# The seven merged products of a four-block scheme, laid between the plain row tiles of the group before them, with bank sums started from copies instead of added at the eviction

## The chip, the cores and the metric

The kernel runs on one core of a Trainium2 chip. The metric is the device time of one execution in microseconds (us), median over runs. The engines are named as in the profile: PE (TensorE matmul) and PEld (its weight load), DVE (VectorE), ACT (ScalarE), POOL (GpSimd) and SP (SyncE, which here only issues transfers). Banks are PSUM banks of 128 x 512 fp32.

## The reference

One layer of a hybrid decoder on 256 tokens (and 16 meta tokens in front of them) with model width 2048 and hidden width 8192, all in fp32:

```
proj  = rmsnorm(x) @ w_in                      # q, k, v, gates of two branches
y     = sigmoid(gate_fox) * (fox(proj) @ w_o_fox) + sigmoid(gate_gla) * (gla(proj) @ w_o_gla)
h     = x + y @ w_out                          # "gemm of y" below
x2    = rmsnorm(h)
out   = h + square(relu(x2 @ w1)) @ w2         # the MLP: ff1 makes a, ff2 gathers into h
```

## The kernel before

**Arithmetic.** An fp32 product is made of three matmuls in fp32r. A tile of weights comes by DMA from SP's queue as `raw` (512 KB, 128 x 1024, a ring of five buffers). ACT casts it into the upper half of a `w` tile (the hi part), DVE subtracts to make the lower half (the lo part), and PE multiplies hi by the token tile's hi and lo parts, then lo by its hi part. `cut` is this pair of ACT and DVE instructions; `w` is a ring of five tiles for the whole kernel, so a cast waits until PE has done with the tile that lies five cuts back in its slot. Token tiles (`x2`, `a`) are kept already split.

**Stages.** The part that the change touches starts at 752 us: the out-projection of `y` in 16 columns j (`gemm2`), each with `add_residual` and the making of `x2`. Then the MLP in four groups of 2048 hidden columns. A group has two ff1 pairs (`x2` to hidden columns of `a`) and two ff2 pairs (`a` gathered into `h`). The last group has one ff1 pair, followed by `token_rows`, a last `hidden` and ordinary column products. That makes 13 pairs, counted here as index 0 to 12: index % 4 is 0 or 1 for ff1, 2 or 3 for ff2.

**A pair** (`two_wide`) makes two row tiles f = 0, 1 of 512 output columns for the two token tiles t = 0, 1 in four banks: `by`, `bx` for f = 0, `bz`, `bv` for f = 1. For the first four of the 16 k blocks it uses a scheme of seven products instead of eight: their weights are differences of weight tiles (made on DVE by `merge` into `ha` and `hb`) and their token operands are sums of token tiles (`s_x2`, `s_a`, made by `token_sums`). The other twelve k blocks are twelve `plain` tiles, two products of six matmuls each. One pair is 186 matmuls of 128 x 512. Three intermediate sums (`m1`, `m5`, `u3`) are copied out of banks by `snap` and added on DVE when the row tile is evicted. In the program's text the seven products and the plain tiles `plain(1,4)`, `plain(1,6)`, `plain(0,4)`, `plain(0,6)` of the same pair alternate, then eight plain tiles follow.

**Evictions.** `hidden` (ff1) adds the kept sum (`added`, DVE), applies relu and square (ACT), transposes 32 x 32 blocks on DVE and sends the result through memory: four DMAs `there<-turn`, one DMA `turn<-there`, then a split into `a` (`turned_parts`, one ACT cast and one DVE subtract per token half). For the first row tile of a group it also makes `s_a`. These steps are put behind numbers of later weight cuts: `behind.append([slot, ...])` counts them down at each cut (`made`). The `turn` tiles are a pool of two buffers, here called A and B; the temporary of `token_sums` is one of them too. `gathered` (ff2) adds into `ht`, and in the last groups turns as well.

**Order.** A scheduler works from the program's text, the waits and its own table of costs, and writes a fixed order for each engine; the DMA issues of a queue go out in order, and a waiting instruction holds whatever is behind it on its engine.

Of the kernel before, what the change touches and what calls it, by code (L numbers as in the profile page):

```python
# [16 lines left out]
P = 128  # L17
# [55 lines left out]
def trunk(ctx: ExitStack, tc: tile.TileContext, hT, w_small, w_all, consts, w_alpha2, out):  # L73
# [162 lines left out]
    def turn(rows, then, both, into=None, slot=10, reload=None):  # L236
# [13 lines left out]
        behind.append([slot, away])  # L250
        if reload:
            behind.append([slot, reload])
        behind.append([slot + 2, lambda: nc.scalar.dma_start(back, there)])
        behind.append([slot + 4, lambda: then(back.rearrange("p (c t j r) -> p j t c r", c=4, t=2, r=32))])
# [770 lines left out]

    acc2 = gat.tile([P, NT], F32, tag="acc", name="acc2", bufs=1)
    for j in range(KT):
# [7 lines left out]
        if j == 4:  # L1035
            g4 = gained[:, 0 : 4 * NT].rearrange("p (j t c r) -> p j t c r", j=4, t=2, r=32)
            token_sums(s_x2, lambda i, t: g4[:, 2 * i : 2 * i + 2, t], gained[:, 4 * NT :])
        if j % 4 == 3:
            nc.scalar.dma_start(kept[:, NT * (j - 3) : NT * (j + 1)].rearrange("p (j t) -> p j t", t=NT),
                                ht[:, j - 3 : j + 1, :])  # L1040
    r2 = gat.tile([P, 2], F32, name="r2", bufs=1)
# [30 lines left out]
    def added(dst, ps, more):  # L1072
        if more is None:
            return ps
        nc.vector.tensor_tensor(dst, ps, more, op=ALU.add)
        return dst

    def hidden(a, b, pt, more=(None, None), slot=10):
# [4 lines left out]
        def part(t):  # L1083
            nc.scalar.activation(u[:, t, :], added(u[:, t, :], pt[t], more[t]), AF.Relu, scale=r2[:, t : t + 1])
# [9 lines left out]
        turn([lambda t=t: part(t) for t in range(2)], ready, both, slot=slot)  # L1094

    def gathered(g, b, pt, more):
# [3 lines left out]
        for r, ps, m in zip(rs, pt, more):  # L1100
            if g == 0:
                if m is None:
                    nc.scalar.copy(r, cells(ps))
                else:
                    nc.vector.tensor_tensor(r, cells(ps), cells(m), op=ALU.add)
            else:
                nc.vector.tensor_tensor(r, cells(ps), r, op=ALU.add)
                if m is not None:
                    nc.vector.tensor_tensor(r, cells(m), r, op=ALU.add)
# [11 lines left out]
        turn([lambda r=r: r for r in rs], add, turn_tile(), reload=reload)  # L1121

    def fetch(dst, c0, k0):
        nc.sync.dma_start(dst.rearrange("p (c k m) -> p c k m", k=2, m=P),
                          w_all[c0 : c0 + 4, :, k0 * P : (k0 + 2) * P].rearrange("c p (k m) -> p c k m", m=P))

    def fetched(c0, k0):
        raw = wp.tile([P, HK * P], F32, tag="raw", name=nm("raw"), bufs=RAW)
        fetch(raw, c0, k0)
        return raw  # L1130

    def cut(raw):
        hi, lo = (t.rearrange("p k m -> p (k m)").rearrange("p (k c m) -> p k c m", k=2, m=P) for t in pair())
        r = raw.rearrange("p (c k m) -> p k c m", k=2, m=P)
        copied = nc.scalar.copy(hi, r).ins  # L1135
        nc.vector.tensor_tensor(lo, r, hi.bitcast(F32), op=ALU.subtract)  # L1136
        made(copied, 1)
        return [t.rearrange("p k c m -> p k (c m)") for t in (hi, lo)]

    def two_wide(x, sums, evict, between=None, split_order=False):  # L1140

        f1 = chunk[0]
        f2 = f1 + 4
        chunk[0] += 8
        begun = set()
        even = len(pairs_done) % 2 == 0
        pairs_done.append(f1)
        pools = (px, px, px, px) if even else (pg, pg, pg, px)
# [44 lines left out]
        if between:  # L1193
            between()
# [219 lines left out]
```

## Time and profile before

| what | value |
|---|---|
| median of three runs (1529.9, 1529.77, 1533.42) | 1529.9 us |
| time of the profiled execution | 1535.58 us |
| its span, from the first to the last instruction | 1533.9 us |
| mean granted clock of TensorE | 0.995 |
| gemm of `y`, by the starts of matmuls | 752.10 to 837.44 us |
| the 13 pairs (2422 matmuls of 128 x 512) | 837.44 to 1388.61 us |
| `token_rows` and the columns of the last group from `x2` | 1388.61 to 1431.4 us |
| the columns of the last group from `a`, and the end | 1431.4 to 1533.9 us |

In a row of groups of instructions the columns are: line, engine, operation, out<-in, shapes, how often; then busy us in total, mean ns of one; then the idle time of the engine just before them and what ended it. A timeline row gives start, length, engine, line, operation, and in brackets an idle time before it with the instruction whose end released it. A matmul of 128 x 512 has a record of 0.38 us, though the next one starts 0.22 us after it: PE overlaps them, so the pace is read from starts.

### The profile page before, as it was taken

How to read it: one execution, taken by the hardware profiler on the slowest of the kernel's cores; microseconds unless marked ns; L12 is line 12 of the kernel's file. 1: busy time of each engine (PE TensorE's matmuls, PEld its weight loads, DVE VectorE, ACT ScalarE, POOL GpSimd, SP SyncE). 2: the span in 40 equal slices, each digit the busy share in tenths (PEclk: the TensorE clock that was granted, in tenths of full speed). 3: DMA queues.
4: the chain of work that ended last, by engine and by line, in shares of the span. 5: the costliest groups of instructions: out<-in, count | busy, mean ns of one | idle time of the engine just before them, and what ended most of it. 6: DMA issues, size and time to landing. Idle time of an engine off the chain costs nothing.

```text
span 1533.9 us, 22711 instructions
## 1 busy us (share of the span) xinstructions
PE 1513.7 (99%) x8536; PEld 1340.6 (87%) x8536; DVE 1110.9 (72%) x1515; ACT 837.0 (55%) x1213; POOL 126.1 (8%) x198
## 2 busy tenths in 40 slices
PE   9999999999999999999999999999999999999997
PEld 8999999999998888888998878888788888888897
DVE  7898858586665454546788788777887788786765
ACT  7766444555555434444666466556654665455563
POOL 5012010021101000000011000000000000110022
PEclk9999999999999999999999999999999999999999
DMA  9545545465455566666664788667766678888562
GB/s 320 173 151 177 181 163 190 156 216 170 165 169 189 198 209 219 219 206 218 219 236 157 223 274 260 207 199 224 232 216 200 214 243 261 289 259 268 187 201 95
DMA packets 222898, 320.32 MB, mean 209 GB/s; under 512 B 11786, under 2 KB 188564, under 8 KB 222660
## 3 DMA queue, kind: packets, MB, share of 16 engines
q1 hardware_dynamic: 202116, 289.75, 58.0%
q10 hardware_dynamic: 20496, 27.99, 5.7%
q8 instruction: 67, 1.10, 0.3%
q0 software_dynamic: 176, 1.12, 0.2%
q14 instruction: 43, 0.35, 0.1%
HBM read 303.09 MB, written 15.74 MB: 208 GB/s over the span
## 4 chain that ended last, share of the span: by engine, by line
PE 79%; DMA 8%; DVE 6%; ACT 3%; issue 2%; ACTq 0%; POOL 0%; SPq 0%; POOLq 0%; DVEq 0%
PE ps L191 15%; PE ps L192 8%; PE bx L1156 7%; PE pt L226 5%; PE pt L225 5%; PE pt L224 5%; PE bz L1156 5%; PE by L1156 5%; PE bv L1156 5%; PE psa L196 4%; PE psa L200 4%; PE psa L198 4%; DMA raw<-w_all_dram 3%; DMA turn<-there 2%; DVE w L1136 2%
## 5 line engine op out<-in xcount | busy, mean ns | idle before, releaser
L134 DVE TENSOR_TENSOR w<-raw,w 128x1024 fp32r<-128x1024 f32 x222 | 273.1, 1231 | 103.1 <-ACT w L133 97.6
L133 ACT CAST w<-raw 128x1024 fp32r<-128x1024 f32 x222 | 232.6, 1049 | 98.2 <-PE psa L200 31.0
L1136 DVE TENSOR_TENSOR w<-raw,w 128x1024 fp32r<-128x1024 f32 x182 | 222.4, 1241 | 81.7 <-ACT w L1135 79.9
L1135 ACT CAST w<-raw 128x1024 fp32r<-128x1024 f32 x182 | 187.6, 1047 | 114.5 <-PE bx L1156 45.6
L191 PE MATMUL ps<-x,w 128*128 128x512 f32 x607 | 206.0, 383 | 0.0
L178 DVE TENSOR_TENSOR w<-raw,w 128x1024 fp32r<-128x1024 f32 x92 | 113.1, 1230 | 110.7 <-ACT w L177 108.8
L196 PE MATMUL psa<-x,w 128*128 128x272 f32 x640 | 181.7, 285 | 0.0
L200 PE MATMUL psa<-x,w 128*128 128x272 f32 x640 | 179.7, 282 | 0.0
L198 PE MATMUL psa<-x,w 128*128 128x272 f32 x624 | 175.9, 282 | 0.0
L192 PE MATMUL ps<-x,w 128*128 128x256 f32 x607 | 166.6, 274 | 0.0
L177 ACT CAST w<-raw 128x1024 fp32r<-128x1024 f32 x92 | 96.3, 1046 | 119.6 <-PE pt L226 113.2
L191 PEld LDWEIGHTS ps<-x,w 128*128 128x128 f32 x607 | 114.0, 188 | 19.3
L196 PEld LDWEIGHTS psa<-x,w 128*128 128x128 f32 x640 | 120.2, 188 | 0.2
L200 PEld LDWEIGHTS psa<-x,w 128*128 128x128 f32 x640 | 120.2, 188 | 0.1
L198 PEld LDWEIGHTS psa<-x,w 128*128 128x128 f32 x624 | 117.4, 188 | 0.0
L192 PEld LDWEIGHTS ps<-x,w 128*128 128x128 f32 x607 | 114.0, 188 | 0.0
L1135 ACT CAST w<-ha 128x1024 fp32r<-128x1024 f32 x52 | 54.4, 1047 | 78.4 <-DVE ha L1179 63.2
L191 PE MATMUL ps<-y,w 128*128 128x512 f32 x256 | 85.4, 380 | 0.0
L224 PE MATMUL pt<-w,x 128*128 128x512 f32 x224 | 85.2, 381 | 0.0
L225 PE MATMUL pt<-w,x 128*128 128x512 f32 x224 | 85.2, 380 | 0.0
L226 PE MATMUL pt<-w,x 128*128 128x512 f32 x224 | 85.2, 380 | 0.0
L1156 PE MATMUL bx<-w,x 128*128 128x512 f32 x336 | 82.8, 383 | 0.0
(402 smaller groups left out, 3095.6 us busy)
## 6 DMA issues: line engine op xcount, KB each, us to landing
raw<-w_all_dram SPq DMA_DIRECT2D x499, 512.0 KB, 4.4
there<-turn ACTq DMA_DIRECT2D x76, 128.0 KB, 3.5
turn<-there ACTq DMA_DIRECT2D x19, 512.0 KB, 6.3
raw<-w_all_dram SPq DMA_DIRECT2D x26, 256.0 KB, 3.5
ha<-w_all_dram SPq DMA_DIRECT2D x13, 512.0 KB, 6.7
hb<-w_all_dram SPq DMA_DIRECT2D x13, 512.0 KB, 4.3
raw<-w_all_dram SPq DMA_DIRECT2D x8, 384.0 KB, 6.5
h<-hT_dram SPq DMA_DIRECT2D x8, 275.0 KB, 6.5
```

Of the source, the lines that this page charges most:

```text
L133: copied = nc.scalar.copy(hi[:, k, :], r).ins
L134: nc.vector.tensor_tensor(lo[:, k, :], r, hi[:, k, :].bitcast(F32), op=ALU.subtract)
L191: nc.tensor.matmul(steps(ps), hi, steps(row(x)), start=first, stop=False)
L192: nc.tensor.matmul(steps(ps[:, 0:NT]), lo, steps(x[:, 0, :]), start=False, stop=last)
L196: nc.tensor.matmul(steps(ps[:, X_LO]), hi, steps(x_lo[:, k]), start=first, stop=False, skip_group_check=True)
L198: nc.tensor.matmul(steps(ps[:, 0:NA]), lo, steps(x_hi[:, k]), start=False, stop=last and hi is None, skip_group_check=True)
L200: nc.tensor.matmul(steps(ps[:, 0:NA]), hi, steps(x_hi[:, k]), start=False, stop=last, skip_group_check=True)
L224: nc.tensor.matmul(steps(ps), xh, steps(hi), start=(k == 0), stop=False)
L225: nc.tensor.matmul(steps(ps), xh, steps(lo), start=False, stop=False)
L1135: copied = nc.scalar.copy(hi, r).ins
L1136: nc.vector.tensor_tensor(lo, r, hi.bitcast(F32), op=ALU.subtract)
L1156: nc.tensor.matmul(steps(ps), l, steps(r), start=ps.tensor.name not in begun, stop=last and k == 1 and n == 2, skip_group_check=True)
```

## The change

`two_wide` becomes `pair_of`, which returns two lists: the seven steps of the scheme and the twelve plain tiles. A loop runs the plain tiles of one pair, and behind those numbered (2, 3, 4, 6, 8, 9, 10), or (1, 2, 3, 5, 7, 8, 9) where index % 4 is 2, it runs one step of the *next* pair. The first pair's seven steps go behind columns j = 8 to 14 of the gemm of `y`. Bank `y` starts as an ACT copy of bank `x` after the first product; `z` and `v` start as DVE sums of bank `x` and the copy `m5`. The kept sums `m1` and `u3` and the additions at the eviction go. All fetched tiles come from the ring `raw`; merged weights go to a ring `hold` of three. The numbers of cuts behind which an evicted tile is sent, fetched back and split change from 10, 12, 14 to 8, 11, 14 (8, 10, 12 for the last group's f = 1; 5, 7, 9 for 6, 8, 10 at the last `hidden`).

The core of the diff:

```diff
+        def step1():
+            r11, got["12"] = fetched(f1, 0), fetched(f2, 0)
+            w = cut(r11)
+            got["t1"] = merged(got["12"], r11)
+            product("x", own(0, 0), w, True)
+            nc.scalar.copy(bk("y"), bk("x"))
+        def step2():
+            got["22"] = fetched(f2, 2)
+            w = cut(got["t1"])
+            got["t2"] = merged(got["22"], got["t1"])
+            product("v", summed(0), w, True)
+            got["t3"] = merged(got["22"], got["12"])
+            got["m5"] = fp.tile([P, 512], F32, tag="m5", name=nm("m5"))
+            nc.scalar.copy(got["m5"], bk("v"))
+        def step3():
+            product("x", summed(1), cut(got["t2"]))
+            nc.vector.tensor_tensor(bk("z"), bk("x"), got["m5"], op=ALU.add)
+        def step4():
+            w = cut(got["t3"])
+            got["21"] = fetched(f1, 2)
+            got["t4"] = merged(got["21"], got["t2"])
+            product("x", summed(2), w)
+            nc.vector.tensor_tensor(bk("v"), bk("x"), got["m5"], op=ALU.add)
+        def step5():
+            product("z", summed(3), cut(got["22"]))
+        def step6():
+            product("y", own(0, 2), cut(got["21"]))
+        def step7():
+            product("x", own(1, 2), cut(got["t4"]))
...
-            nc.scalar.activation(u[:, t, :], added(u[:, t, :], pt[t], more[t]), AF.Relu, scale=r2[:, t : t + 1])
+            nc.scalar.activation(u[:, t, :], pt[t], AF.Relu, scale=r2[:, t : t + 1])
...
-        nc.vector.tensor_tensor(m5, bx, m5, op=ALU.add)
-        u3 = snap(bx, "u3")
-        evict(1, (bz, bv), (m5, u3))
...
+        at = (1, 2, 3, 5, 7, 8, 9) if index % 4 == 2 else (2, 3, 4, 6, 8, 9, 10)
+        for i, run in enumerate(rest_now):
+            run()
+            if index == 0 and i == 2:
+                norm2()
+            if i in at and steps_next:
+                steps_next[at.index(i)]()
...
-    hidden(a, 2, *token_rows(x2, 1), slot=6)
+    hidden(a, 2, *token_rows(x2, 1), slots=(5, 7, 9))
```

Places in the engines' orders follow. Names carry the scheduler's numbers.

DVE where the first pair is evicted and the second begins, before. L1075 adds the kept sums at the eviction, L240 transposes, L1179 merges weights, L1136 makes lo parts:

```order
L1136 TENSOR_TENSOR w_1245_9021<-ha_1243_9017,w_1245_9021 128x1024
L240 STREAM_TRANSPOSE turn_1227_8926<-turn_1227_8926 128x4x128
L1179 TENSOR_TENSOR ha_1243_9017<-hb_1244_9018,ha_1243_9017 128x1024
L240 STREAM_TRANSPOSE turn_1227_8926<-turn_1227_8926 128x4x128
L1179 TENSOR_TENSOR hb_1244_9018<-raw_1247_9033,hb_1244_9018 128x1024
L1136 TENSOR_TENSOR w_1248_9035<-ha_1243_9017,w_1248_9035 128x1024
L1136 TENSOR_TENSOR w_1251_9049<-raw_1250_9047,w_1251_9049 128x1024
L1179 TENSOR_TENSOR ha_1243_9017<-raw_1247_9033,ha_1243_9017 128x1024
L1075 TENSOR_TENSOR turn_1237_9003<-bz_1193_8682,m5_1201_8712 128x512
L1075 TENSOR_TENSOR turn_1237_9003<-bv_1194_8683,u3_1210_8792 128x512
```

And the same pair boundary on DVE now (L1042 merges, L1036 makes lo parts):

```order
L288 TENSOR_TENSOR a_1238_8940<-turn_1239_8941,a_1238_8940 128x4x128 x2
L1042 TENSOR_TENSOR hold_1278_9207<-raw_1276_9202,hold_1271_9174 128x1024
L1042 TENSOR_TENSOR hold_1280_9216<-raw_1276_9202,raw_1268_9158 128x1024
L1036 TENSOR_TENSOR w_1275_9187<-raw_1274_9185,w_1275_9187 128x1024
L240 STREAM_TRANSPOSE turn_1259_9096<-turn_1259_9096 128x4x128 x2
L1036 TENSOR_TENSOR w_1277_9204<-hold_1271_9174,w_1277_9204 128x1024
L1036 TENSOR_TENSOR w_1283_9222<-raw_1282_9220,w_1283_9222 128x1024
L1042 TENSOR_TENSOR hold_1294_9300<-raw_1293_9298,hold_1278_9207 128x1024
L1036 TENSOR_TENSOR w_1284_9237<-hold_1278_9207,w_1284_9237 128x1024
```

Between two transposed tiles there is no addition of an eviction any more, and the merges stand one to a plain tile.

ACT in the second ff1 pair of the first group (index 1) now. The casts from `hold` and that of `w_1299` are steps 2 to 5 of the following ff2 pair, the others are plain tiles; `s_a` is the operand of steps 2 to 5:

```order
L1035 CAST w_1292_9294<-hold_1280_9216 128x1024
L253 DMA turn_1259_9096<-there_1260_9103 128x1024
L1035 CAST w_1296_9311<-raw_1295_9309 128x1024
L1035 CAST w_1298_9328<-raw_1297_9326 128x1024
L1035 CAST w_1299_9343<-raw_1276_9202 128x1024
L287 CAST a_1238_8940<-turn_1259_9096 128x4x128 x2
L1035 CAST w_1301_9358<-raw_1300_9356 128x1024
L287 CAST s_a_7826<-turn_1270_9167 128x8x128
L1212 ACTIVATE turn_1288_9269<-by_1223_8858,r2_8762 128x512
L1212 ACTIVATE turn_1288_9269<-bx_1222_8851,r2_8762 128x512
L1035 CAST w_1302_9373<-raw_1293_9298 128x1024
```

And PE at the same place now:

```order
L1069 MATMUL bv_1229_8884<-w_1298_9328,x2_1076_7821 128x4x32x4 x5
L1069 MATMUL bz_1235_8921<-w_1301_9358,x2_1076_7821 128x4x32x4
L1069 MATMUL bv_1229_8884<-w_1301_9358,x2_1076_7821 128x4x32x4
L1069 MATMUL bz_1235_8921<-w_1301_9358,x2_1076_7821 128x4x32x4 x5
L1069 MATMUL bv_1229_8884<-w_1301_9358,x2_1076_7821 128x4x32x4 x5
L1069 MATMUL bv_1279_9209<-w_1277_9204,s_a_7826 128x4x32x4 x2
L1069 MATMUL bx_1272_9176<-w_1284_9237,s_a_7826 128x4x32x4 x2
L1069 MATMUL bv_1279_9209<-w_1277_9204,s_a_7826 128x4x32x4 x4
L1069 MATMUL bx_1272_9176<-w_1284_9237,s_a_7826 128x4x32x4 x4
L1069 MATMUL by_1273_9183<-w_1302_9373,a_1238_8940 128x4x32x4 x6
```

The casts of steps 2 to 5 stand several plain tiles ahead of the products that use them: on PE all four steps come behind the plain tile `w_1301`, so their `w` tiles are held until then.

ACT at the end, before: the last `s_a` stands behind the split of the last turned tile of `a`, among the casts of the columns.

```order
L253 DMA turn_1799_12973<-there_1800_12980 128x1024
L280 COPY evb_1823_13152<-ps_1822_13119 128x256
L133 CAST w_1841_13269<-raw_1840_13268 128x1024
L287 CAST a_1734_12500<-turn_1799_12973 128x4x128 x2
L133 CAST w_1843_13274<-raw_1842_13273 128x1024
```

ACT at the end, now:

```order
L287 CAST a_1790_12692<-turn_1805_12809 128x4x128 x2
L133 CAST w_1845_13099<-raw_1844_13098 128x1024
L133 CAST w_1847_13104<-raw_1846_13103 128x1024
L287 CAST s_a_7826<-turn_1825_12946 128x8x128
L1212 ACTIVATE turn_1826_12981<-pt_1807_12821,r2_8762 128x512
L1212 ACTIVATE turn_1826_12981<-pt_1808_12822,r2_8762 128x512
```

The cast of `s_a` now stands ahead of the last row tile's relu, which takes its `turn` tile only after the temporary of `s_a` and the tile behind it have passed through the two buffers.

212 lines of the change are left out of this document (97 added, 115 removed).

## The prediction

> **What bounds the kernel now.** I read the page's busy times and its chain first.
>
> ```profile
> span 1533.9 us, 22711 instructions
> PE 1513.7 (99%) x8536; PEld 1340.6 (87%) x8536; DVE 1110.9 (72%) x1515; ACT 837.0 (55%) x1213; POOL 126.1 (8%) x198
> PE 79%; DMA 8%; DVE 6%; ACT 3%; issue 2%; ACTq 0%; POOL 0%; SPq 0%; POOLq 0%; DVEq 0%
> ```
>
> PE is busy 99% of the span, DVE 72%, ACT 55%. The change takes no matmul away: a pair stays seven products of 6 and twelve plain tiles of 12, 186 matmuls. So it can only win what PE loses between matmuls, and it must be read from the stage that it rearranges. The windows by stage give it (columns: length, then busy us and count of PE, PEld, DVE, ACT, POOL, then granted clock, DMA share, GB/s):
>
> ```profile
> 752.10:837.40 85.30, 85.30 (x514) 77.03 (x513) 69.93 (x92) 49.75 (x78) 11.60 (x13) 1.00 0.65 218
> 837.44:1388.61 551.17, 545.14 (x2425) 454.11 (x2423) 441.13 (x456) 318.37 (x374) 14.55 (x11) 1.00 0.74 234
> ```
>
> The pairs take 551.17 us. At what pace? Starts of matmuls in two stretches:
>
> ```profile
> 870.00 1.48 PE L1156 MATMUL bv<-w,x 128*128 128x512 f32 x6
> 871.32 0.38 PE L1156 MATMUL bz<-w,x 128*128 128x512 f32 x1
> ...
> 999.83 1.50 PE L1156 MATMUL bv<-w,a 128*128 128x512 f32 x6
> 1001.17 1.05 PE L1156 MATMUL bz<-w,a 128*128 128x512 f32 x4
> ```
>
> Six matmuls take 1.32 us in the first (0.2200 each) and 1.34 in the second (0.2233). At 0.2200 the stage's 2422 would take 532.8 us, so 18.3 us are lost. Adding up every distance between starts that is over 0.1 us above the pace gives 11.5 us in stalls; the other 6.8 are the slower pace, which begins with the first stall at 883 us and comes and goes at later stalls.
>
> The largest cluster is in the second pair, at the boundary:
>
> ```profile
> 881.88 1.49 PE L1156 MATMUL bz<-w,x 128*128 128x512 f32 x6
> 884.07 0.49 PE L1156 MATMUL bz<-w,x 128*128 128x512 f32 x1 [0.70 <-ACT w L1135]
> 885.52 1.49 PE L1156 MATMUL bz<-w,x 128*128 128x512 f32 x5 [0.96 <-DVE w L1136]
> 886.80 2.76 PE L1156 MATMUL bx<-w,s_x 128*128 128x512 f32 x6
> 889.36 1.83 PE L1156 MATMUL bv<-w,x 128*128 128x512 f32 x6
> ```
>
> The sixth matmul of the first row starts at 882.98, the next at 884.07: 0.87 us lost; then 885.52 instead of 884.29: 1.23 lost. From 886.80 six matmuls take 2.56 us instead of 1.32: half clock. What is late is said by DVE's rows there:
>
> ```profile
> 881.84 0.69 DVE L1075 TENSOR_TENSOR turn<-bz,m 128x512 f32<-128x512 f32 x1
> 882.45 0.69 DVE L1075 TENSOR_TENSOR turn<-bv,u 128x512 f32<-128x512 f32 x1
> 883.10 1.23 DVE L1136 TENSOR_TENSOR w<-ha,w 128x1024 fp32r<-128x1024 f32 x1
> 884.25 1.22 DVE L1136 TENSOR_TENSOR w<-raw,w 128x1024 fp32r<-128x1024 f32 x1
> 885.38 1.22 DVE L1179 TENSOR_TENSOR ha<-raw,ha 128x1024 f32<-128x1024 f32 x1
> ```
>
> DVE works without a gap: the additions of the eviction, merges and transposes come in one burst, and the lo part for `bz` stands behind them. Over the whole stage DVE has 441 of 551 us to do, so this is bunching, not a shortage.
>
> **The change, part by part.** *The boundary bursts.* Per pair, DVE loses two of four bank additions (0.69 each) and the rest, with the four merges (1.2 each), is spread one to a plain tile. A plain tile costs PE 2.64 us; DVE's lo part plus a merge is 2.4. In the new orders the steady pairs stand on PE as whole sixes, hi and lo ready together. I credit the full 11.5 us: -11.5. If half of it stays, as when a transposed tile meets a merge, -6. The four additions or copies per pair that move into banks cost ACT and DVE no more than the rows they replace:
>
> ```profile
> L1173 ACT COPY m<-bv 128x512 f32<-128x512 f32 x13 | 7.5, 578 | 0.0
> L1179 DVE TENSOR_TENSOR ha<-raw,ha 128x1024 f32<-128x1024 f32 x25 | 30.5, 1220 | 0.0
> ```
>
> A copy from bank to bank has no row; taken as 578 ns, at most twice that, it lies beside the 2.64 us of the plain tile that PE runs before the bank is used: 0.
>
> *The gemm of `y`.* The first pair's steps lie in seven of its columns. PE then has 85.30/16 + 6 x 0.22 = 6.65 us a column; DVE has 69.93/16 = 4.4, with a lo part and at times a merge 6.0 to 6.8. Nearly even, with one column's weights ahead: 0.4 us, between 0 and 3.
>
> *A new wait, at index 1, 5 and 9.* There the following ff2 pair's steps 2 to 5 need `s_a`. It is made so in the trace of before:
>
> ```profile
> 909.83 1.29 DVE L288 TENSOR_TENSOR a<-turn,a 128x512 fp32r<-128x512 f32 x2 [1.35 <-ACT a L287]
> 912.44 0.42 DVE L1012 TENSOR_TENSOR turn<-turn 128x256 f32<-128x256 f32 x1
> 914.02 1.05 ACT L287 CAST s_a<-turn 128x1024 fp32r<-128x1024 f32 x1 [1.81 <-DVE turn L1015]
> 915.11 1.23 DVE L288 TENSOR_TENSOR s_a<-turn,s_a 128x1024 fp32r<-128x1024 f32 x1
> ```
>
> Its temporary is a `turn` tile, and there are two: one holds the first row tile, the other the second until that is split. So `s_a` comes only after the split of f = 1. Before, it was needed a whole pair later; now its products are wanted within index 1. Their four `w` tiles are cut early (the order shows it) and wait, and they hold four of the five slots. The plain tiles run through the fifth: the cast of `w_1301` waits until PE has done with `w_1298`, the very tile ahead of it on PE. PE then has nothing. Durations of a cast and a lo part:
>
> ```profile
> L1135 ACT CAST w<-raw 128x1024 fp32r<-128x1024 f32 x182 | 187.6, 1047 | 114.5 <-PE bx L1156 45.6
> L1136 DVE TENSOR_TENSOR w<-raw,w 128x1024 fp32r<-128x1024 f32 x182 | 222.4, 1241 | 81.7 <-ACT w L1135 79.9
> ```
>
> PE waits 1.05 + 0.2 (hand-over) = 1.25 for the hi part. Two hi matmuls start, then the lo part is waited for: 1.24 + 0.2 - 0.44 = 1.0, and 1.24 with the tail of a sum (0.42) ahead on DVE. Then come lo of `s_a` (0.15), lo of step 6 behind it (0.35) and the cast behind relu, square and the `m5` copy (0.5). Sum 3.5 us, three times: +10.5. The floor is 2.0 each (only the shared slot, 1.25 + 0.8), the ceiling 4.4 (the transfer `there` landing 0.9 late as well).
>
> *The clock behind it.* At 883 to 886 us pieces of 0.87 and 1.23 us sufficed for half clock, at 1.24 us per six matmuls, 1.45 lost in all. The new wait has 2.5 us of pieces in about 3 us. At another boundary a single piece of 1.18 (929.93 instead of 928.75) did nothing to the six behind it:
>
> ```profile
> 927.21 1.76 PE L1156 MATMUL bz<-w,a 128*128 128x512 f32 x7
> 929.93 1.38 PE L1156 MATMUL bz<-w,a 128*128 128x512 f32 x5 [0.96 <-DVE w L1136]
> 931.15 1.49 PE L1156 MATMUL bx<-w,s_a 128*128 128x512 f32 x6
> ```
>
> Of three chances I count one and a half, at 1.7: +2.5 (0 to 5). The Trainium skill, in "TensorE: Matmul & The Clock Gate", "Why this matters for your kernels", asks for "No PE-idle gaps >~3µs between matmul bursts", so pieces like these should cost no clock; by it this term is 0 and the sum 2.5 us lower. The row at 886.80 speaks against it: half clock after two pieces of 2.1 us together.
>
> *The end.* Before, PE waits once there; the rows are PE's wait, the timeline of ACT, and the window behind the wait:
>
> ```profile
> PE ps L191 <- DVE a L288: 3.3, 1, 3.3
> ...
> 1418.81 1.27 ACT L1084 ACTIVATE turn<-pt,r 128x512 f32<-128x512 f32 x2
> 1428.76 0.34 ACTq L253 DMA_DIRECT2D turn<-there  x1
> 1435.51 1.14 ACT L287 CAST a<-turn 128x512 fp32r<-128x512 f32 x2 [4.99 <-DMA turn<-there]
> ...
> 1436.50:1443.00 6.50, 5.49 (x17) 4.71 (x18) 6.33 (x13) 4.20 (x7) 0.00 (x0) 0.50 0.28 88
> ```
>
> 3.3 us of waiting and then half clock for over 6 us, which costs 3 more. Now the last `s_a`, which nobody uses, stands ahead of the relu on ACT, and its temporary ahead of the relu's tile in the ring. Against that the slots come one cut earlier and f = 1 turns earlier. I take +1.5; -3 if the wait shrinks by half its idle time and its clock, +3 if the relu falls a column (5.3 us) behind and half of that is hidden.
>
> *The pace.* Of 6.8 us, a quarter is won: fewer stalls, and the first comes some 22 us later: -1.7, between 0 and -6.8.
>
> *Other queues.* The transfers are the same 512 KB tiles in almost the same order on SP's queue, DMA share 0.74 in the stage; raw tiles are held longer by steps (up to three of five), covered while PE's tile of 2.64 us exceeds what 0.74 of the queue takes of that, 2.0. On ACT's queue the four `there` issues stand between casts as before. If that cover goes, a raw landing (4.4 us) shows, in the upper end of the range.
>
> Sum: -11.5 + 0.4 + 10.5 + 2.5 + 1.5 - 1.7 = +1.7 us. On the profiled execution's own 1535.6 that is 1537.3; its own time lies 5.7 us above the median of 1529.9, so against the median I predict 1531.6. A difference within 0.3% (4.6 us) is about what a measurement of this kernel can't tell from none.
>
> **Rivals.** *Slower: the held `w` slots decide.* Same place, index 1, 5 and 9. If the turned tile lands late, `s_a` is later still and PE stands with all five slots held: 4.4 of waiting and 1.7 of clock are 6.1 each, 18.3 instead of 13.0; with +3 at the end and 0.4, -11.5 and no gain of pace, that is +10, and 1538 in its middle (+8). It decides from about 5.5 us a place. For it: landings of up to 4.1 us waited for in this stage:
>
> ```profile
> ACT a L287 <- DMA turn<-there: 21.3, 11, 3.1
> ACT w L1135 <- DMA there<-turn: 21.1, 6, 4.1
> ```
>
> Against: in most pairs those waits were ACT's and PE saw nothing of them.
>
> *Faster: the new waits stay at their floor, or PE fills them.* Waits of 2.0 each without half clock are 6.0; with -11.5, 0.4, an end unchanged and a pace regained by half (-3.4), that is -8.5, some 1522. For it: only three pairs of thirteen have the conflict, and the other boundaries lose their bursts. Against: the shared slot follows from the order and doesn't depend on luck.
>
> *No matter at all.* The bursts only move: DVE's 441 us are still due, and each stall removed comes back elsewhere, while the pace stays at 0.2233: within 2 us of before. For it, the pattern of single hi matmuls ahead of groups of five on PE in index 1. Against: DVE sheds 1.4 us a pair.
>
> *The gate by the page's rule.* Pieces below 3 us cost no clock: then 0 in place of 2.5, sum -0.8, 1529.1. The skill's section says so; the row at 886.80 differs, so I give it little.
>
> **How the numbers follow.** My forecast, the waits near 3.5 with the gains nearly cancelled, 0.28; the bursts only moving 0.07; the page's rule 0.05; together 0.40 for within 0.3%. The slower rival 0.30. The faster one 0.30. The likeliest is 1531.6. The range takes in the faster case a little past its middle and the slower one to its sum: 1521.0 to 1541.0. My own case alone: 1527 to 1536.
>
> **What would show it.** In the profile after: boundaries of index 2, 3, 6, 7, 10 and 11 without waits of PE on lo parts; no bank additions between transposes; in index 1, 5 and 9 a wait on a hi part of about 1.2 us followed by one on a lo part, both ahead of products with `s_a`, and the cast's own wait on PE; ACT's cast of the last `s_a` ahead of the relu, and PE's wait for `a` at the end some 1 to 2 us longer. I am wrong if PE never waits in index 1, 5 and 9, if the gemm of `y` grows by more than its 42 matmuls x 0.22 = 9.2 us, or if the waits at the steady boundaries remain.

## The result, and the profile after

The changed kernel takes 1543.93 us (median; 1541.75 to 1548.5) against 1529.84 (1529.54 to 1533.42): the ratio is 1.0091, with a 95% interval of 1.0063 to 1.0119. It is slower by 14 us. The forecast was 1531.6 in a range of 1521 to 1541.

The profiled execution took 1544.94 us. The page of after:

```profile
span 1543.2 us, 22665 instructions
PE 1515.9 (98%) x8536; PEld 1340.1 (87%) x8536; DVE 1089.0 (71%) x1489; ACT 837.1 (54%) x1206; POOL 124.7 (8%) x198
```

DVE has 22 us less to do, as the removed additions say, and PE stands still longer. Gemm of `y` and the pairs must be taken as one stage now, since they overlap. First before, then after, in windows of this stage and, for after, of the two behind it:

```profile
752.10:1388.61 636.51, 630.49 (x2937) 531.18 (x2935) 511.06 (x548) 368.17 (x451) 26.16 (x24) 1.00 0.73 232
```

```profile
751.57:1399.22 647.65, 633.88 (x2937) 531.85 (x2935) 490.85 (x523) 368.58 (x446) 27.45 (x24) 0.99 0.71 229
1399.22:1442.00 42.78, 42.78 (x226) 37.27 (x225) 28.43 (x38) 23.58 (x32) 0.00 (x0) 1.00 0.71 230
1442.00:1543.20 101.20, 90.12 (x590) 82.72 (x588) 60.73 (x97) 53.71 (x91) 17.76 (x19) 0.95 0.47 160
```

The stage is 11.1 us longer. The two behind it take 42.78 and 101.2 us, where before had 42.8 and 102.5: the end gained 1.3. PE's waits over the whole span name the engines:

```profile
PE by L1069 <- DVE w L1036: 5.6, 5, 1.9
PE bz L1069 <- ACT w L1035: 4.4, 4, 1.1
PE bz L1069 <- DVE w L1036: 3.8, 4, 1.0
PE ps L191 <- DVE a L288: 3.0, 1, 3.0
...
```

From the starts of the matmuls of this stage I make three sums for each kernel: *waits* (distances that exceed the pace by over 0.08 us), *half clock* (distances of about 0.427 us), and *pace* (what the other matmuls of 512 columns take over 0.2200 us each):

| kernel | waits | half clock | pace | stage, us |
|---|---|---|---|---|
| before | 9.8 | 1.7 | 6.9 | 636.5 |
| after | 17.7 | 3.3 | 8.4 | 647.7 |

So the 11.1 us are, but for rounding, 7.9 of waits, 1.6 of half clock and 1.5 of pace. Where the waits are, in PE's timeline of after:

```profile
860.74 0.93 PE L1069 MATMUL by<-w,x 128*128 128x512 f32 x3 [0.90 <-DVE w L1036]
...
884.46 0.49 PE L1069 MATMUL bz<-w,x 128*128 128x512 f32 x1 [1.00 <-ACT w L1035]
885.72 1.41 PE L1069 MATMUL bz<-w,x 128*128 128x512 f32 x5 [0.77 <-DVE w L1036]
...
896.45 1.36 PE L1069 MATMUL by<-w,x 128*128 128x512 f32 x5 [1.04 <-DVE w L1036]
...
905.21 2.04 PE L1069 MATMUL by<-w,x 128*128 128x512 f32 x5 [1.89 <-DVE w L1036]
...
913.70 1.38 PE L1069 MATMUL by<-w,x 128*128 128x512 f32 x5 [0.94 <-DVE w L1036]
...
1264.86 0.49 PE L1069 MATMUL bz<-w,x 128*128 128x512 f32 x1 [1.14 <-ACT w L1035]
...
1266.58 1.66 PE L1069 MATMUL bz<-w,x 128*128 128x512 f32 x5 [1.01 <-DVE w L1036]
1268.04 2.33 PE L1069 MATMUL bv<-w,x 128*128 128x512 f32 x5
```

The last three rows are index 9. A wait on a hi part of 1.14 and one on a lo part of 1.01 us, the very pair that the prediction described, stands also at 925 (index 1) and 1096 us (index 5), in the same two numbers. In starts each is 2.7 us, 8.1 in all. One other wait of 1.1 us is at 998 (index 3). The rest, 8.2 us of waits and the half clock behind 905, falls in the first two pairs (index 0 and 1), where nothing of the kind was forecast; in the gemm of `y` itself PE waits nowhere. At the boundaries of all later pairs there is no wait left.

What DVE waited for in those two pairs (its timeline; L1042 merges two weight tiles):

```profile
858.32 1.23 DVE L1042 TENSOR_TENSOR hold<-raw,hold 128x1024 f32<-128x1024 f32 x1 [4.01 <-DMA raw<-w_all_dram]
...
894.03 1.23 DVE L1042 TENSOR_TENSOR hold<-raw,raw 128x1024 f32<-128x1024 f32 x1 [4.14 <-DMA raw<-w_all_dram]
...
901.66 1.22 DVE L1042 TENSOR_TENSOR hold<-raw,hold 128x1024 f32<-128x1024 f32 x1 [1.79 <-DMA raw<-w_all_dram]
...
910.15 1.23 DVE L1042 TENSOR_TENSOR hold<-raw,hold 128x1024 f32<-128x1024 f32 x1 [1.54 <-DMA raw<-w_all_dram]
```

Each late `by` of PE stands behind such a merge: the merge waits for a raw tile that has not landed, and the lo part of a plain tile, whose hi part PE has already begun to use, stands behind the merge on DVE. The merge at 858 waits ahead of `spread`. Why raw tiles were late from 883 us on is in SP's queue:

```profile
867.84 0.37 SPq L1196 DMA_DIRECT2D line<-r  x1
875.63 0.33 SPq L1197 DMA_DIRECT2D r2b<-line  x1
876.06 6.12 SPq L1028 DMA_DIRECT2D raw<-w_all_dram  x5
```

`spread` sends the norm's 256 factors to memory in pieces of 4 bytes (`line<-r`) and fetches them back spread over the partitions (`r2b<-line`). The second waits for the first to land, 7.7 us, and all raw tiles wait behind it. Before has the same two transfers in the same queue, with one raw tile between them:

```profile
855.29 0.37 SPq L1062 DMA_DIRECT2D line<-r  x1
856.90 0.37 SPq L1124 DMA_DIRECT2D raw<-w_all_dram  x1
865.28 0.34 SPq L1063 DMA_DIRECT2D r2b<-line  x1
```

### The profile page after: what moved, and what is told of

Read it like the earlier page. It is cut to its first block, busy times and chain, and to the rows that moved or that the text cites. A ratio compares the mean times of both kernels' runs of the same rounds, so it can differ in the third digit from the quotient of the medians.

```text
span 1543.2 us, 22665 instructions
## 1 busy us (share of the span) xinstructions
PE 1515.9 (98%) x8536; PEld 1340.1 (87%) x8536; DVE 1089.0 (71%) x1489; ACT 837.1 (54%) x1206; POOL 124.7 (8%) x198
## 4 chain that ended last, share of the span: by engine, by line
PE 85%; DMA 6%; DVE 5%; issue 2%; ACT 1%; ACTq 0%; SPq 0%; POOL 0%; POOLq 0%; DVEq 0%
PE ps L191 15%; PE bx L1069 9%; PE ps L192 8%; PE bv L1069 7%; PE bz L1069 7%; PE by L1069 6%; PE pt L226 5%; PE pt L225 5%; PE pt L224 5%; PE psa L196 4%; PE psa L200 4%; PE psa L198 4%; DMA raw<-w_all_dram 3%; DVE w L1036 1%; PE ps L460 1%
## 5 line engine op out<-in xcount | busy, mean ns | idle before, releaser
L134 DVE TENSOR_TENSOR w<-raw,w 128x1024 fp32r<-128x1024 f32 x222 | 273.1, 1233 | 100.6 <-ACT w L133 98.6
L1035 ACT CAST w<-raw 128x1024 fp32r<-128x1024 f32 x195 | 202.8, 1047 | 158.2 <-PE bx L1069 54.8
L133 ACT CAST w<-raw 128x1024 fp32r<-128x1024 f32 x222 | 232.5, 1049 | 96.3 <-PE psa L200 31.0
L1036 DVE TENSOR_TENSOR w<-raw,w 128x1024 fp32r<-128x1024 f32 x195 | 234.8, 1222 | 67.1 <-ACT w L1035 65.9
L178 DVE TENSOR_TENSOR w<-raw,w 128x1024 fp32r<-128x1024 f32 x92 | 113.7, 1236 | 113.9 <-ACT w L177 111.1
L177 ACT CAST w<-raw 128x1024 fp32r<-128x1024 f32 x92 | 96.3, 1047 | 122.9 <-PE pt L226 115.5
L1069 PE MATMUL bx<-w,x 128*128 128x512 f32 x336 | 86.2, 387 | 0.0
L1069 PE MATMUL by<-w,x 128*128 128x512 f32 x294 | 76.5, 388 | 4.8 <-DVE w L1036 4.8
```

The source lines that it names most:

```text
L133: copied = nc.scalar.copy(hi[:, k, :], r).ins
L134: nc.vector.tensor_tensor(lo[:, k, :], r, hi[:, k, :].bitcast(F32), op=ALU.subtract)
L1069: nc.tensor.matmul(steps(ps), l, steps(r), start=start and k == 0 and i == 0, stop=False, skip_group_check=True)
```

## The experiments

Three causes were to be told apart: the *hole* that `spread` makes in the raw stream, the raw *ring* of five that plain tiles now share with the steps (before, `ha` and `hb` were two more streaming buffers), and the *held slots* of `w` at index 1, 5 and 9. All times are against the kernel before in the same comparison.

**e1: spread's transfers on POOL's queue, in the changed kernel.**

```diff
-        nc.sync.dma_start(line.rearrange("o (t p) -> p (o t)", t=2), r2)
-        nc.sync.dma_start(r2b, line.to_broadcast([P, NT]))
+        nc.gpsimd.dma_start(line.rearrange("o (t p) -> p (o t)", t=2), r2)
+        nc.gpsimd.dma_start(r2b, line.to_broadcast([P, NT]))
```

> The changed kernel with the two transfers of spread (line<-r2, r2b<-line) on POOL's queue instead of SP's; all other orders are the same. Theory Q (SP's queue stands still while r2b waits for the landing of line, about 8 to 11 us, and the raw ring of five runs dry): the stalls at 883, 895, 903 and 912 us (2.3 + 1.3 + 3.9 with half clock + 1.2 = 8.7 us) go, time 1544 - 8 = about 1536; raw transfers are issued without a hole between 865 and 876. Rival R (the ring of five is too short because the steps hold raw tiles, whatever the queue does): the stalls stay, time 1541 or more. The waits at 924, 1094 and 1263 us stay by both.

1543.66 us, ratio 1.0073 (1.0046 to 1.0099): no gain that the intervals show. Waits stay at 17.6 us. The wait at 883 is gone, those at 862 to 914 us are as large. Theory Q in this form falls. But the DMA view of e1 between 871 and 882 us (busy tenths and GB/s in 40 slices) shows something else:

```profile
DMA  0001000333559900089691457002300130135734
GB/s 0 0 0 4 0 0 0 15 74 138 171 186 171 26 0 0 0 11 15 48 78 22 45 60 30 22 4 45 22 0 19 34 37 15 15 30 26 30 108 171
```

Raw tiles were issued at 872.1, 874.7, 877.0 and 878.2 us and landed 10 to 11 us later, where the median of the execution is 4.1; apart from a stretch of up to 186 GB/s between 873 and 875 us, little moved until `line<-r` landed at 880. Before shows the same in SP's queue: its raw tile of 856.90, issued behind `line<-r`, landed after 10.5 us. This suggests that the hole is made by the transfer of small pieces, whatever queue it is in: theory H.

**e2: the same edit in the kernel before.**

> The kernel before with the same two transfers on POOL's queue. Theory Q: the cluster at 883 us of before (3.9 us with half clock), which the prediction gave to a burst on DVE, was the same hole in SP's queue (856.9 to 865.3 us): it goes, 1526 to 1527. Rival B (burst on DVE): it stays, 1530, no change.

1530.88 us, ratio 0.9982 (0.9965 to 0.9998). The cluster of waits at 883 us is gone from the trace; twelve matmuls run there in one piece:

```profile
881.22 3.14 PE L1156 MATMUL bz<-w,x 128*128 128x512 f32 x12
```

Waits fall from 9.8 to 5.6 us and half clock from 1.7 to 0.4, while the pace of the profiled execution was 14.0 us. The burst on DVE is in both traces: the same instructions follow each other with hardly a gap. Before it begins 2.5 us later; first before, then e2:

```profile
872.98 0.68 DVE L1075 TENSOR_TENSOR turn<-by,m 128x512 f32<-128x512 f32 x1
870.45 0.68 DVE L1075 TENSOR_TENSOR turn<-by,m 128x512 f32<-128x512 f32 x1
```

So it was the delay by `spread`'s hole that made the burst cost 3.9 us of PE's time; without the delay the same burst costs PE nothing there. And of the 5.6 us left in e2 only about half stand behind such a burst, the second row of PE's list (which counts idle time, and so less than the distances between starts):

```profile
PE bx L1156 <- ACT u L1173: 1.6, 2, 0.9
PE bz L1156 <- DVE w L1136: 1.5, 2, 0.9
PE bx L1156 <- DVE m L1198: 0.2, 1, 0.2
```

In the first and the third row PE waits until a bank has been copied by ACT or summed up by DVE, which happens inside a pair. The change takes these waits away too; the prediction's reading of the 11.5 us did not name them.

**e3: the temporary of `token_sums` in its own turned tile**, in the half that has already been sent.

```diff
-                temp = turn_tile()
-                token_sums(s_a, lambda i, t: back[:, 2 * i : 2 * i + 2, t], temp[:, 0 : 8 * P])
+                token_sums(s_a, lambda i, t: back[:, 2 * i : 2 * i + 2, t], both[:, 0 : 8 * P])
```

> The changed kernel with the temporary of token_sums in the sending half of its own turned tile instead of a tile of the ring of two, so that s_a no longer waits for the split of the second row tile. Theory W (the held w slots at index 1, 5 and 9): the waits at 924, 1094 and 1263 us (2.9 + 2.9 + 2.8, and 1.6 of half clock) go, time 1544 - 8 to 10 = 1534 to 1536. Rival (the w ring of five is too short for steps among plain tiles in any case): less than 3 us gained, over 1541. The first group's stalls up to 912 us stay.

1534.16 us, ratio 1.0018 (0.9996 to 1.0040): 9.8 us below the changed kernel by the medians, 0.73% by the ratios, as theory W says. The pairs of waits at index 1, 5 and 9 are gone. The first group's waits are there and new ones behind them; PE's list for the stage:

```profile
PE by L1069 <- DVE w L1036: 9.6, 5, 3.1
PE bz L1069 <- DVE w L1036: 0.8, 1, 0.8
...
```

**e4: e1 and e3 together.**

> Both edits of the changed kernel together. If the two causes are separate and complete, the gains add up: 1544 - 8 - 9 = about 1527, below before. If what is left is the pace of 0.2233 and other waits, 1530 to 1534.

1532.89 us, ratio 0.9996 (0.9975 to 1.0016): no gain over e3 that the intervals show, and not the sum of two gains. A merge of the third pair, in DVE's timeline of e4, says what remained:

```profile
940.96 1.23 DVE L1042 TENSOR_TENSOR hold<-raw,raw 128x1024 f32<-128x1024 f32 x1 [7.47 <-DMA raw<-w_all_dram]
```

**e5: r11 and r12 streamed into the ring `hold`, merges in place**, in the changed kernel, so that seven or eight buffers stream again. `held()` takes a tile of that ring, and the third argument of `merged` says where its result goes.

```diff
-            r11, got["12"] = fetched(f1, 0), fetched(f2, 0)
+            r11, got["12"] = fetched(f1, 0, held()), fetched(f2, 0, held())
...
-            got["t1"] = merged(got["12"], r11)
+            got["t1"] = merged(got["12"], r11, r11)
...
-            got["t3"] = merged(got["22"], got["12"])
+            got["t3"] = merged(got["22"], got["12"], got["12"])
...
-            got["t4"] = merged(got["21"], got["t2"])
+            got["t4"] = merged(got["21"], got["t2"], got["t2"])
```

> The changed kernel with the first two fetched tiles of a pair's steps (r11, r12) streamed into the hold ring of three and the merges t1, t3, t4 made in place there, so that the raw ring of five is left to the plain tiles and two of the step tiles; the memory is the same. Theory R (the ring of five shared with the steps is too short: a merge on DVE waits for its raw tile to land and holds the lo part behind it): the waits at 860 us and at 895 to 912 us go or shrink to a third, 6 to 8 us off, so 4 to 6 us above before. Rival W alone (only the held w slots matter): no gain, 11 to 12 us above before. The waits at 924, 1094 and 1263 us stay by both.

1537.65 us, ratio 1.0051 (1.0027 to 1.0074). The waits at 860, 896 and 913 are gone, those at 883 (the hole) and 905 stay, and the three of the held slots stay, as expected. It stands 7.5 us above before, where 4 to 6 were expected.

**e6 and e7: the ring and the sums, without and with POOL's queue.** The edits are those of e5 and e3, and of e1.

> The same ring edit and the temporary of token_sums in its own turned tile. Theories R and W together: the waits of e3 at 860, 898, 907, 941 and 998 us (12 us) shrink to 4 or less: 1.5 us above before (e3) less 7 = 5 us below before. If e3's waits came from the order of DVE and not from the ring, it stays where e3 was, 1 to 3 us above before.

> The ring edit, the sums edit and the two transfers of spread on POOL's queue. As e6, with 1 to 2 us less because SP's queue no longer stands: 6 to 7 us below before. If the queue is of no account where the ring is long enough, equal to e6 within 1 us.

e6: 1530.16 us, ratio 0.9984 (0.9959 to 1.0009); waits 6.3 us, all between 882 and 905 us. By the ratio it stands 2.4 us below before, where 5 were expected. e7: 1524.18 us, ratio 0.9962 (0.9935 to 0.9989); one wait is left, 3.5 us at 899, and the waits are 2.5 us fewer than in e6. The rest of the 6 us between the two medians is not waits, and their intervals overlap: what the queue is worth by itself stays unsettled.

**e8: the changed kernel without spread's transfers** (`r2b` is filled by one POOL copy from `r2`, which leaves out the transposition of the factor; other engines' orders are the same).

```diff
-        line = dram.tile([1, NT], F32, name="line")
-        nc.sync.dma_start(line.rearrange("o (t p) -> p (o t)", t=2), r2)
-        nc.sync.dma_start(r2b, line.to_broadcast([P, NT]))
+        nc.gpsimd.tensor_copy(r2b, r2[:, 0:1].to_broadcast([P, NT]))
```

> The changed kernel without the transfers of spread: r2b is filled by one copy on POOL from r2, which leaves out the transposition of the norm's factor, so the last group's values differ. All other orders are the same. Theory H (not the queue but the 1 KB transfer of 4-byte pieces itself stops the streams: in e1 the DMA engines moved 0 to 54 GB/s between 871 and 881 us with raw tiles issued): the waits from 883 to 912 us go, 5 to 7 us above before. Rival R (ring): they stay for the most part, 10 us or more above before.

1534.91 us, ratio 1.0027 (1.0006 to 1.0048). Between 880 and 930 us PE's timeline has two waits, and they are those of the held slots:

```profile
920.25 0.49 PE L1069 MATMUL bz<-w,x 128*128 128x512 f32 x1 [1.14 <-ACT w L1035]
...
921.96 1.40 PE L1069 MATMUL bz<-w,x 128*128 128x512 f32 x5 [1.01 <-DVE w L1036]
```

The whole chain from 883 to 913 us is gone with a transfer of 1 KB and its way back, where e1, which only moved them, kept most of it: theory H holds. The wait at 860 us, which comes ahead of `spread`, is the ring's and stays. It is 3.4 us in this execution against 1.2 in the changed kernel's, and two of some 0.5 us are new (1078 and 1119), so that the waits of this one trace sum to only 2.8 us less; the 9 us between the medians are of all its runs.

**e9 and e10: no such transfer, with the edits of e5 and e3 (e9) and in the kernel before (e10).** `r2b` is made on chip: matmuls of ones with the parts of the sums, then the root on DVE over 256 columns. e10 has the edit of e3 as well.

```diff
-                nc.tensor.matmul(steps(ps), part[:, P * t : P * t + P], steps(unit), start=(n == 0), stop=(n == 1))
+                nc.tensor.matmul(steps(ps[:, 0:NT]), part[:, P * t : P * t + P], steps(unit[:, 0:NT]), start=(n == 0), stop=(n == 1))
+            if t == 0:
+                for n, part in enumerate((hi, lo)):
+                    nc.tensor.matmul(ps[:, NT:512], unit[:, 0:P], part, start=(n == 0), stop=(n == 1))
+                nc.scalar.copy(r2b, ps[:, NT:512])
...
-        nc.sync.dma_start(line.rearrange("o (t p) -> p (o t)", t=2), r2)
-        nc.sync.dma_start(r2b, line.to_broadcast([P, NT]))
+        v, r = (gat.tile([P, NT], F32, tag="hsq", name=nm("rsb")) for _ in range(2))
+        root(r2b, r2b, v, r, 1.0 / D)
```

> The changed kernel with the ring and sums edits, and r2b made without memory: two matmuls of ones with the sums' parts spread them over the partitions, and the root is taken there on DVE, so that the transfers of 4-byte pieces are gone. Theory H: no hole in the raw stream between 870 and 881 us, so e7's last wait (3.5 us at 899 us, behind a turned tile that landed late) goes too: 8 to 10 us below before, 1521. Rival: the wait at 899 us is a burst on DVE of the new order itself and stays: 5 to 6 us below before, as e7.

> The kernel before with the same two edits that are not the change (sums in the own turned tile, r2b made on PE), to see what the interleaving alone is worth once its side effects are gone. If the interleaving removes the boundary waits (5.5 us left in e2) it stands 5 us above e9, 3 to 4 us below before. If the interleaving is worth nothing, it is level with e9.

e9: 1513.87 us, ratio 0.9892 (0.9865 to 0.9918). e10: 1521.58 us, ratio 0.9935 (0.9911 to 0.9958). The windows of the stage, e9 and then e10:

```profile
752.91:1371.67 618.76, 618.76 (x2938) 531.76 (x2937) 498.92 (x535) 369.74 (x447) 28.36 (x24) 1.00 0.75 240
```

```profile
752.01:1380.72 628.71, 625.29 (x2938) 530.49 (x2937) 513.68 (x560) 369.43 (x452) 27.21 (x24) 1.00 0.74 235
```

In e9 PE is busy in all of its 618.76 us; e10 has 5.3 us of waits. PE's list for e10:

```profile
PE bz L1158 <- ACT w L1137: 1.7, 1, 1.7
PE bx L1158 <- ACT u L1175: 1.5, 3, 0.7
PE bx L1158 <- DVE m L1200: 0.2, 1, 0.2
```

The first row is at the start of the last pair, where ACT's cast waits for a merge in DVE's burst; the others are as in e2. So the change removes what before so mended still loses, of which about half is the burst that the prediction named. e9 is read for its time alone: an inherited bank loses part of the sum that it begins from (told below).

**e11 and e12: the spread sums in a full bank of their own, with and without the ring edit.**

```diff
+        ps = bank(pg, "pn")
+        nc.tensor.matmul(ps, unit[:, 0:P], parts, start=True, stop=True)
+        nc.scalar.copy(r2b, ps[:, 0:NT])
+        nc.vector.tensor_tensor(r2b, ps[:, NT:512], r2b, op=ALU.add)
```

> As e9, but the spread sums are made by one matmul of 512 columns in a bank of its own (sum of hi beside sum of lo), so that each bank that a later pair begins from a copy has been written by matmuls in all of its columns; in e9 one had been written in 256 only and lost the copied sum in the rest. The time should be e9's: no wait of PE among the pairs, 1513 to 1516, 1.0 to 1.2% below before. If e9 was quick because of what it left out, it stands at e7's 1524.

> As e11 without the ring edit: all fetched tiles of the steps come from the raw ring of five, as in the changed kernel. If the short ring costs by itself, waits on merges remain at 860, 941 and 998 us (e4: 3.8 + 3.6 + 1.7 us): 6 to 9 us above e11. If the ring mattered only behind the hole in the raw stream, level with e11 within 2 us.

e11: 1522.08 us, ratio 0.9935 (0.9914 to 0.9957). e12: 1533.67 us, ratio 1.0008 (0.9985 to 1.0032), with 10.6 us of waits at 858, 905, 938 and 996 us. So the short ring costs 11 us by itself, without the hole. Beside the hole the same edit is worth 5 to 6 us by the ratios (e5 against the changed kernel, e6 against e3, e7 against e4). In e11 PE has no wait at all in the stage, as in e9, and yet it is 8 us slower, where it was expected level. The windows are 626.94 against 618.76 us, and the difference is in every matmul; PE's timeline of e9 and then of e11:

```profile
1099.75 1.48 PE L1074 MATMUL bx<-w,a 128*128 128x512 f32 x6
1101.07 1.48 PE L1074 MATMUL bz<-w,a 128*128 128x512 f32 x6
```

```profile
1099.65 1.50 PE L1074 MATMUL by<-w,a 128*128 128x512 f32 x6
1100.99 2.39 PE L1074 MATMUL bx<-w,a 128*128 128x512 f32 x10
```

Six matmuls take 1.32 us in e9 (0.2200 each, flat) and 1.34 in e11 (0.2233, in turns of 0.222 and 0.225). It is not the lost sum that makes e9 quick: e7 and e14 run at 0.2200 too, for most of the stage.

**e13 and e14: what sets the pace.** The single matmul of 512 columns in e11 becomes four, or two, of 256.

```diff
-        nc.tensor.matmul(ps, unit[:, 0:P], parts, start=True, stop=True)
+        for n, part in enumerate((hi, lo, hi, lo)):
+            nc.tensor.matmul(ps[:, NT * (n // 2) : NT * (n // 2) + NT], unit[:, 0:P], part, start=(n == 0), stop=(n == 3),
+                             skip_group_check=True)
```

> As e11, with the matmul of 512 columns that spreads the sums replaced by four of 256 columns over the same bank (three of them in a row on PE); nothing else moves. e9 and e11 have no wait of PE among the pairs and differ by 8 us in the pace alone (0.2200 after a run of four matmuls of 256 columns at 861 us in e9, 0.2233 throughout in e11). Theory P (the pace is a phase between weight loads and matmuls that a run of shorter matmuls or a stall resets): the pace falls to 0.2200 behind it, 1513 to 1516. Rival (the pace depends on where the program or the data lie, or on the chip): 0.2233 stays or comes by chance, 1520 to 1524, or differs from run to run.

> As e13 with two matmuls of 256 columns that stand apart on PE. By theory P a single short matmul resets the phase too, or it needs several: in e9 a pair of them at 859 us left the slow pace as it was. I expect the slow pace, 1520 to 1524, as e11; with theory P in its simple form 1513 to 1516.

e13: 1520.74 us, ratio 0.9923 (0.9895 to 0.9951); pace 8.4 us, slow throughout, with three short matmuls in a row at 860 us. e14: 1518.29 us, ratio 0.9911 (0.9878 to 0.9944); slow until a wait of 1.9 us at 899, at 0.2200 behind it, where 1520 to 1524 us were expected. Theory P in its simple form falls: short matmuls do not reset the pace reliably; waits do change it, not always. Nor is it the chip alone: e1 to e4 ran on one chip, with 3.1 to 16.1 us of pace. What decides is open. The three sums again:

| kernel | waits | half clock | pace | stage, us |
|---|---|---|---|---|
| e1 | 17.6 | 4.3 | 4.4 | 644.6 |
| e2 | 5.6 | 0.4 | 14.0 | 638.1 |
| e3 | 13.4 | 2.5 | 16.1 | 650.3 |
| e4 | 13.9 | 2.7 | 3.1 | 637.9 |
| e5 | 13.9 | 0 | 4.4 | 636.6 |
| e6 | 6.3 | 1.0 | 8.4 | 633.9 |
| e7 | 3.8 | 1.4 | 1.3 | 624.8 |
| e8 | 14.9 | 2.5 | 9.9 | 645.5 |
| e9 | 0 | 0 | 0.7 | 618.8 |
| e10 | 5.3 | 0 | 5.4 | 628.7 |
| e11 | 0 | 0 | 8.4 | 626.9 |
| e12 | 10.6 | 2.7 | 7.4 | 639.1 |
| e13 | 0 | 0 | 8.4 | 627.2 |
| e14 | 2.0 | 0 | 1.3 | 621.8 |

The waits say what an edit did; a single execution's time says it only after the pace is taken off.

## Why the prediction was wrong

By its own steps, with what the profile of after measured on the profiled execution:

| step | forecast | measured |
|---|---|---|
| boundary bursts go | -11.5 | -11.4 |
| gemm of `y`, first two pairs | +0.4 | +9.9 (8.2 waits, 1.65 half clock) |
| new waits at index 1, 5, 9 | +10.5 | +8.1 |
| half clock behind them | +2.5 | +1.6 |
| a wait at 998 us | 0 | +1.1 |
| the end | +1.5 | -1.3 |
| pace | -1.7 | +1.5 |

The right column sums to +9.5, and the profiled executions differ by 9.4 (1544.94 against 1535.58). In the first row the 11.4 are all that before loses, with some 4 us of `spread`'s hole in them; the changed kernel pays for the hole again in the second row. The wait at 998 is the ring's: it is gone in e5, e6, e7, e9 and e11, and stays in e3, e4, e8 and e12.

*The step that failed is "Other queues".* It gave the raw tiles no term in the sum; measured, the first two pairs lost 9.9 us, all of it outside the gemm of `y`, whose own 0.4 held. The step said that raw tiles held longer by the steps were covered, since PE's tile of 2.64 us exceeds the queue's 2.0. That compared mean rates and left out two things. First, the change took away two streaming buffers: r11 and r12 went from `ha`, `hb` to the ring of five, and a step's merge that waits for its tile blocks the lo parts of plain tiles on DVE. e12 against e11 sizes this without the hole: 11 us. Secondly, the two transfers of `spread` stood in the rows of the queue that I read past. They stop the stream for some 8 us, and a stage that uses 0.71 to 0.75 of the DMA time refills slowly. e8 sizes this against the changed kernel: ratio 1.0027 instead of 1.0091, some 10 us. The two sizes don't add, since each was taken with other edits in place; in the trace of the changed kernel both causes together are the 9.9 of the row. Before bore the same hole with 4 us of loss (e2). That it had more tiles ahead may be why, but this is not shown: e6, with as many buffers, still loses 6.3 us of waits there.

*The burst at 883 us was half read.* The prediction put this cluster, 3.9 of its 11.5 us, down to additions and merges piling up on DVE. DVE was busy nearly without a gap there, so the reading fitted; yet e2 moves two DMA issues to another queue, DVE is as full, and the cluster is gone, because the burst starts 2.5 us earlier. Of the other waits of before, 5.6 us in e2 and 5.3 in e10, about half stand behind a burst at a boundary (1.5 of 3.3 and 1.7 of 3.4 us in PE's lists). That the full 11.5 were won was partly luck: the copies of kept banks, on which PE also waited, went with the change. Where the ring is short, a wait at a boundary can come back by another way: e3, e4 and e12 wait 2.2 to 3.6 us at the start of index 2, behind a merge whose tile has not landed.

*The new wait was right in mechanism, place and nearly in size.* 1.14 and 1.01 us, three times to the hundredth, with ACT's cast released by PE and `s_a` 3.6 us behind it:

```profile
1263.76 1.04 ACT L1035 CAST w<-raw 128x1024 fp32r<-128x1024 f32 x1 [0.58 <-PE bv L1069]
1267.36 1.05 ACT L287 CAST s_a<-turn 128x1024 fp32r<-128x1024 f32 x1 [2.55 <-DVE turn L1015]
```

The terms behind the lo part (lo of `s_a`, step 6, relu) came to nearly nothing, so 2.7 and not 3.5 each. e3 takes the cause away and the waits go, for about 10 us.

*The gate.* Of three identical waits one, at index 9, was followed by eight matmuls at 0.427 us, as was the single wait of 1.89 us at 905; the forecast counted one and a half of the three. By the Trainium skill, "TensorE: Matmul & The Clock Gate", "Why this matters for your kernels", none should have been, since no gap reaches 3 us: here 1.14 and 1.01 us with two matmuls between them sufficed, and 1.89 us alone. The same page says under "Part 1: The HAM clock gate" that the window is free-running; that the same wait costs the clock once and twice not is in keeping with it, but no run here shows the window.

*The end* went better. `s_a` stands ahead of the relu, as the order said, but the turned tile is fetched and lands in time for a wait of 3.0 instead of 3.3 us and a shorter half clock:

```profile
1426.95 1.05 ACT L287 CAST s_a<-turn 128x1024 fp32r<-128x1024 f32 x1 [1.66 <-DVE turn L1015]
1427.90 1.26 ACT L1212 ACTIVATE turn<-pt,r 128x512 f32<-128x512 f32 x2
...
1440.20 0.34 ACTq L253 DMA_DIRECT2D turn<-there  x1
...
1445.80 1.14 ACT L287 CAST a<-turn 128x512 fp32r<-128x512 f32 x2 [3.84 <-DMA turn<-there]
```

*The base.* The forecast put its sum on the median, 1529.9, though the profiled execution stood 5.7 us above it; after's stands 1.0 above its own. These 4.7 us are the difference between the 9.4 us of the profiled executions and the 14.1 of the medians; 9.4 on the median of before would have been 1539.3. Such distances are ordinary here: in one comparison the kernel before ran from 1522.87 to 1538.74 us. Its median in the later comparisons is 1530.2 to 1532.7, so 1529.84, from four runs, may be a little low. The pace, which differs by up to 15 us between the traces here, is large enough to make them; that it does was not shown, since only profiled executions have traces.

*The signs and the rivals.* Neither of the first and the last sign by which the prediction wanted to be refuted came: PE waited in index 1, 5 and 9, and the steady boundaries were clear. The gemm of `y` grew by 9.8 us instead of 9.2, at a slower pace and without a wait. No sign looked at the landing of raw tiles. The slower rival, 1538, came nearest to the time, but by luck: its held slots cost 8.1 us of waits and 1.6 of half clock, not 18.3.

*What the change is worth once its side effects are gone* depends on the pace. With the ring, the sums and the spread mended, PE has no wait left where before with the sums and the spread mended (e10) has 5.3 us. e9 beats e10 by 7.7 us, where the stage is 9.9 us shorter: 5.3 of waits and 4.7 of pace. e11 has e10's ratio, 0.9935: it saves the waits and runs all the way at 0.2233. e11, e13 and e14 are 0.7 to 0.9% below before; of e11's gain, what e10 shows for the kernel before alone is as much.

## What to carry to other kernels

Where steps are moved between others, count the buffers that each stream had before and has after, and look down each DMA queue for a transfer that waits for another: a mean DMA share of 0.7 hides both a shortened ring and a hole of 8 us. A wait on an engine that is busy all the time may come from work that began late, behind a transfer, so move the transfer before blaming the engine. Compare kernels by the waits in their traces as well as by times, where the time of one kernel varies by as much as the change is worth.

## What the runs showed of the hardware

- A transfer of 1 KB in pieces of 4 bytes took 7.7 us to land (9.2 on POOL's queue, e1), and meanwhile 512 KB transfers took 10 to 11 us instead of a median of 4.1 (e1, on another queue), and 10.5 (before, on the same queue).
- The same stream of matmuls of 128 x 512 ran at 0.2200, 0.2233 or 0.2283 us each (e9; e11; e3 from 1000 us on), at the same granted clock of 1.00. It keeps a pace for hundreds of matmuls and changes it mostly at a wait. The largest sum of it in a trace here is 16.1 us (e3).
- In e9 a bank whose last matmuls had written 256 of its 512 columns was begun by a copy and added to without a start flag, and the output was off by a relative 0.049. With the bank written in full (e11) nothing was lost, nor in e10, which writes the same half bank but begins no bank of its pairs from a copy. That half of the copied sum is what was lost is inferred from these three. It is what the Trainium skill says in "PSUM — Partial Sum Buffer", "The four PSUM rules": writes of VectorE and ScalarE neither set nor clear the bits that decide between adding and overwriting. The change rests on every inherited bank having been written in full by matmuls.
